# Norm statistics: squares added up over the feature tiles on GpSimd, one-column products, and the context's norm placed behind the latents' first products

## The chip, the cores and the metric

The kernel runs on one core of one Trainium2 chip. The metric is the device time of one execution in microseconds (us), lower is better. TensorE (PE) multiplies, VectorE (DVE), ScalarE (ACT) and GpSimd (POOL) do the element work, and each has its own in-order instruction queue; the queues of SyncE (SP), ACT and POOL also issue transfers.

## What is computed

Two layers of a diffusion trunk over 512 latent tokens and 256 context tokens, d_model 1024. Each layer has three token mixers behind one input projection, one output projection, and then a dense SwiGLU (layer 0) or an expert SwiGLU (layer 1). A modulated RMSNorm stands ahead of the input projection and ahead of the SwiGLU:

```
def rmsnorm(x, g):
    return x * lax.rsqrt(jnp.mean(jnp.square(x), axis=-1, keepdims=True) + EPS) * g
hl  = modulate(rmsnorm(x, norm1[l]), sh1, sc1);  hc  = modulate(rmsnorm(ctx, norm1[l]), csh1, csc1)
out_l, out_c = token_mixers(hl, hc, w_in[l], ..., w_out[l], ...)
x   = x + g1 * out_l;                            ctx = ctx + cg1 * out_c      # context in layer 0 alone
hl2 = modulate(rmsnorm(x, norm2[l]), sh2, sc2);  hc2 = modulate(rmsnorm(ctx, norm2[l]), csh2, csc2)
x   = x + g2 * channel_mixer(hl2, ...);          ctx = ctx + cg2 * channel_mixer(hc2, ...)
```

Shifts, scales and gates come from `w_mod` (12 groups of 512 columns a layer, called modulation groups here).

## The kernel before

The residual stream lies transposed: eight tiles `xr0` to `xr7` of 128 features by 768 tokens, the latents in columns 0 to 511 and the context in 512 to 767. Every fp32 product is made of three products of split operands: `hi` is a rounded copy (ACT, L207) and `lo` the rest, `raw - hi` (DVE, L208). So each 512 KB block of weights is loaded by SP into `raw`, split by ACT and DVE, and then used by PE in the lines L215 to L217. The buffers of `raw`, `hi` and `lo` rotate, three to five each, so a split also waits until the products of an older block are done.

There are two places that matter here, and both are in or behind layer 0.

**The tail of layer 0** (`tail`, 447 to 543 us). For the latents, then for the context: eight times (m = 0 to 7) load and split a block of `wout`, 24 products, and the residual update of `xr` on DVE (L687). Then `modnorm`: `stats` squares the eight `xr` tiles (odd ones on DVE in L337, even ones on ACT in L339), each square goes through a product with ones (L341) into PSUM, then a copy (L344), transposes (L231), a sum (L347), a root on DVE in 12 tiny instructions (`rsq`, L239 to L246), a diagonal (L352) and a product that spreads the root over the partitions (L357). After that come eight times a scaling (`ht`, DVE L362), `hh` (ACT L367) and `hl` (DVE L368), which are the split operands of the next products. The latents' norm is issued behind the latents' products and so runs on DVE and ACT while PE makes the context's.

**The feed-forward part** (`ffn`). Its blocks f = 0 and f = 1 make the latents' products of both blocks first and then the context's; later blocks do both at once. Beside them DVE makes modulation groups for later (`mod_acc`, L296). In the last chunk the down products (`wd4`, 18 matmuls for each of d = 0 to 7, residual update in L789) are made for the latents first and then for the context, each with its `modnorm` behind it; these norms are those of layer 1, and `project` of layer 1 begins with group 1 (four token tiles of the latents, 24 matmuls each, L221 to L223) and the channels (L215 to L217, latents and context).

What sets the order inside a queue is the order of the program text and the scheduler's priorities; each engine's queue is in order, so an instruction that waits holds up all behind it.

## Time and profile before

| | |
|---|---|
| median of 3 runs | 2162.6 us (2160.61 to 2163.68) |
| profiled execution | 2161.2 us |
| its span, first to last instruction | 2159.5 us, so 1.7 us lie around it |
| PE busy | 2027.9 us, 94% |
| DVE, ACT, POOL busy | 65%, 46%, 8% |
| granted TensorE clock, mean | 0.977 |

PE is busy nearly everywhere, so time is to be had where PE stands still or runs at a lower granted clock, and from products that are not made at all.

### The profile page before, as it was taken

How to read it: one execution, taken by the hardware profiler on the slowest of the kernel's cores; microseconds unless marked ns; L12 is line 12 of the kernel's file. 1: busy time of each engine (PE TensorE's matmuls, PEld its weight loads, DVE VectorE, ACT ScalarE, POOL GpSimd, SP SyncE). 2: the span in 40 equal slices, each digit the busy share in tenths (PEclk: the TensorE clock that was granted, in tenths of full speed). 3: DMA queues.
4: the chain of work that ended last, by engine and by line, in shares of the span. 5: the costliest groups of instructions: out<-in, count | busy, mean ns of one | idle time of the engine just before them, and what ended most of it. 6: DMA issues, size and time to landing. Idle time of an engine off the chain costs nothing. (4 is left out here: it accounts for less than half of the span.)

```text
span 2159.5 us, 33553 instructions
## 1 busy us (share of the span) xinstructions
PE 2027.9 (94%) x12470; PEld 1648.4 (76%) x12470; DVE 1401.9 (65%) x2501; ACT 990.2 (46%) x1728; POOL 179.9 (8%) x246
## 2 busy tenths in 40 slices
PE   6999899989999999999989999999889999999995
PEld 2988766767788888888858987778567777777774
DVE  4859845765885724242366599676676787766776
ACT  3665374533322212122235655754365576645554
POOL 0000231200000000000000004120110000001011
PEclk9999999999999999999989999999899999999998
DMA  7232543162654615131213324034597799667783
GB/s 271 91 121 85 184 144 129 39 198 62 203 204 137 200 35 200 30 98 58 91 48 92 120 81 127 27 104 150 172 308 269 257 350 325 217 218 250 238 291 118
DMA packets 120752, 342.45 MB, mean 159 GB/s; under 512 B 13104, under 2 KB 34592, under 8 KB 120576
## 3 DMA queue, kind: packets, MB, share of 16 engines
q1 hardware_dynamic: 80064, 271.75, 37.8%
q0 software_dynamic: 15248, 49.97, 6.9%
q10 hardware_dynamic: 25264, 18.42, 2.8%
q8 instruction: 106, 1.74, 0.3%
q14 instruction: 70, 0.57, 0.1%
HBM read 304.95 MB, written 35.14 MB: 157 GB/s over the span
## 5 line engine op out<-in xcount | busy, mean ns | idle before, releaser
L207 ACT ACTIVATE hi<-raw 128x1024 fp32r<-128x1024 f32 (+3 forms) x444 | 427.2, 987 | 332.5 <-PE ps L216 262.4
L208 DVE TENSOR_TENSOR lo<-raw,hi 128x1024 fp32r<-128x1024 f32 (+3 forms) x444 | 495.0, 1134 | 92.4 <-ACT hi L207 79.6
L217 PE MATMUL ps<-hh,lo 128*128 128x512 f32 (+1 forms) x1040 | 353.9, 340 | 2.5 <-DVE lo L208 2.5
L215 PE MATMUL ps<-hh,hi 128*128 128x512 f32 (+1 forms) x1040 | 355.1, 341 | 1.0 <-ACT hi L207 0.5
L216 PE MATMUL ps<-hl,hi 128*128 128x512 f32 (+1 forms) x1040 | 354.2, 341 | 0.0
L215 PEld LDWEIGHTS ps<-hh,hi 128*128 128x128 f32 x1040 | 198.1, 191 | 24.9 <-issue 1.7
L217 PEld LDWEIGHTS ps<-hh,lo 128*128 128x128 f32 x1040 | 198.0, 190 | 24.4 <-DVE lo L208 3.0
L216 PEld LDWEIGHTS ps<-hl,hi 128*128 128x128 f32 x1040 | 198.1, 191 | 21.4
L223 PE MATMUL ps<-lo,xh 128*128 128x512 f32 (+1 forms) x384 | 150.6, 392 | 9.5 <-DVE lo L208 4.6
L221 PE MATMUL ps<-hi,xh 128*128 128x512 f32 (+1 forms) x384 | 146.1, 380 | 2.2 <-ACT hi L207 2.2
L222 PE MATMUL ps<-hi,xl 128*128 128x512 f32 (+1 forms) x384 | 144.9, 377 | 0.0
L1273 DVE TENSOR_TENSOR sg<-sg,ps 128x512 f32<-128x512 f32 (+1 forms) x44 | 24.3, 553 | 154.7 <-PE ps L217 154.7
L216 PE MATMUL ps<-gl,hi 128*128 128x256 f32 (+1 forms) x352 | 119.4, 339 | 0.0
L215 PE MATMUL ps<-gh,hi 128*128 128x256 f32 (+1 forms) x352 | 118.9, 338 | 0.0
L217 PE MATMUL ps<-gh,lo 128*128 128x256 f32 (+1 forms) x352 | 118.5, 337 | 0.0
L223 PEld LDWEIGHTS ps<-lo,xh 128*128 128x128 f32 x384 | 72.4, 189 | 37.6 <-DVE lo L208 15.6
L221 PE MATMUL ps<-hi,hh 128*128 128x400 f32 (+2 forms) x272 | 92.2, 339 | 2.5 <-DVE ht L362 1.4
L223 PE MATMUL ps<-lo,hh 128*128 128x400 f32 (+2 forms) x272 | 89.0, 329 | 0.0
L222 PE MATMUL ps<-hi,hl 128*128 128x400 f32 (+2 forms) x272 | 88.9, 327 | 0.0
L1515 DVE TENSOR_REDUCE a_st<-S 128x1 f32<-128x768 f32 (+1 forms) x80 | 66.2, 844 | 33.9 <-PE S L1514 33.5
L296 DVE SCALAR_TENSOR_TENSOR macc<-mraw,sT,macc 128x512 f32<-128x512 f32 x112 | 80.0, 747 | 12.0 <-DMA mraw<-wmod 11.3
L1516 ACT ACTIVATE a_p<-S,a_st 128x768 f32<-128x768 f32 (+1 forms) x80 | 65.2, 817 | 45.8 <-DVE a_st L1515 40.5
(557 smaller groups left out, 4099.9 us busy)
## 6 DMA issues: line engine op xcount, KB each, us to landing
raw<-wmg SPq DMA_DIRECT2D x176, 512.0 KB
raw<-wmd SPq DMA_DIRECT2D x80, 512.0 KB
raw<-wmod SPq DMA_DIRECT2D x52, 512.0 KB
raw<-wgu SPq DMA_DIRECT2D x44, 512.0 KB
mraw<-wmod SPq DMA_DIRECT2D x44, 512.0 KB
raw<-wout SPq DMA_DIRECT2D x32, 512.0 KB
raw<-wt SPq DMA_DIRECT2D x24, 512.0 KB
raw<-wd SPq DMA_DIRECT2D x32, 256.0 KB
```

The lines of the kernel that those rows point to most:

```text
L207: self.nc.scalar.activation(hi, src, AF.Copy)
L208: self.nc.vector.tensor_sub(lo, src, hi.bitcast(F32))
L215: mm(out, wh, xh, start=start, stop=False)
L216: mm(out, wh, xl, start=False, stop=False)
L217: mm(out, wl, xh, start=False, stop=stop)
L221: mm(out, xh, wh, start=start, stop=False)
L222: mm(out, xl, wh, start=False, stop=False)
L223: mm(out, xh, wl, start=False, stop=stop)
L296: nc.vector.scalar_tensor_tensor(a, w, c, a, op0=OP.mult, op1=OP.add)
L1273: nc.vector.tensor_mul(s, s, pu)
L1515: nc.vector.tensor_reduce(st[:, 0, c + i:c + i + 1], s[:, :n], axis=AX.X, op=OP.min)
L1516: nc.scalar.activation(P[:, :n], s[:, :n], AF.Exp, bias=st[:, 0, c + i:c + i + 1], scale=-1.0, accum_out=st[:, 1, c + i:c + i + 1])
```

## The change

Squares all run on ACT (`square`), and GpSimd adds them up over the eight feature tiles into an accumulator (`nac0` for the latents, with the last square alone in `nac1`; `nacc` for the context). `rms` then makes one product of one column for each tile of 128 tokens and accumulator (eight for the latents, two for the context) and goes on with the root, the diagonal and the spreading product. Of the context's weight blocks (`wout` and `wd4`), three in four have their `lo` made on GpSimd. The context's norm of the tail is placed in `ffn` behind the first latents products, that of the feed-forward's end in `project` behind token tile 1 of group 1, with x read back from DRAM (`xres`). The latents' norm for layer 1 goes in two pieces of 256 columns. The writes of `xres` go from GpSimd's queue to SP's and ACT's. Modulation group 10 of layer 0 is no longer made on PE within the attention but as one more group on DVE in `ffn`.

```diff
+    def square(self, pool, acc, xs, k):
+        nc = self.nc
+        if k == 0 or k == 7 and len(acc) > 1:
+            nc.scalar.activation(acc[k // 7], xs, AF.Square)
+            return
+        sq = pool.tile([128, 512], F32, name="sq")[:, :xs.shape[-1]]
+        nc.scalar.activation(sq, xs, AF.Square)
+        nc.gpsimd.tensor_add(acc[0], acc[0], sq)
+
+    def rms(self, pool, acc, n, b, dg=None):
...
+        for t in range(m):
+            for j, a in enumerate(acc):
+                nc.tensor.matmul(q[:, t:t + 1], a[:, t * 128:t * 128 + 128], self.C("ones")[:, 0:1], start=j == 0, stop=j == len(acc) - 1)
+        self.rsq(pool, q[:, :m], [128, m], 1.0 / 1024, EPS, ss, "n")
...
+    def modnorm(self, pool, hh, hl, x, s, o, n, gain, modc, sh0, rs, w):
+        for c in range(0, n, w):
+            for k in range(8):
+                t = pool.tile([128, 512], F32, name="ht")[:, :w]
+                self.scaled(t, x, s, o + c, w, gain, rs[:, c:c + w], k)
+                self.shifted(t, hh, hl, s, o + c, w, modc, sh0, k)
...
-            attention = mix.attention(at, cat, list(range(4, 11)) if l == 0 else [])
+            attention = mix.attention(at, cat, list(range(4, 10)) if l == 0 else [])
...
+    def context():
+        sqs = [cv.tile([128, 4, 2, 64], F32, name="sq").rearrange("p t h d -> p (t h d)") for _ in range(2)]
...
+            nc.scalar.dma_start(xs[-1][:, :n * CTX].rearrange("p (d c) -> p d c", c=CTX), k.xsrc[1][:, d:d + n, LAT:])
+        rs = k.rms(cv, k.acc, CTX, "pg", sqs[1])
...
+                    if l == 1 and i == 1 and t == 1:
+                        context()
...
-                wh, wl = k.weight(A["wout"][l, m].rearrange("p k n -> p (k n)"))
+                wh, wl = k.weight(A["wout"][l, m].rearrange("p k n -> p (k n)"), eng=nc.gpsimd if s and m % 4 < 3 else None)
...
+                if not last:
+                    k.square(np_, acc, xm, m)
...
-        done, sums = [], {2: 4, 4: 4, 7: 4, 11: 4}
+        done, sums = [], {2: 4, 4: 4, 6: 4, 10: 4, 12: 2}
...
-            for i, g in ((0, 11), (1, 2), (1, 3), (1, 0), (1, 1), (1, 4), (1, 5), (1, 6), (1, 7), (1, 8), (1, 9)):
+            for i, g in ((0, 10), (0, 11), (1, 2), (1, 3), (1, 0), (1, 1), (1, 4), (1, 5), (1, 6), (1, 7), (1, 8), (1, 9)):
...
-                    up(fs, SEGS[:1])
+                    up(fs[:1], SEGS[:1])
+                    rs = k.rms(fp, k.acc, CTX, "pn", mp.tile([128, 512], F32, name="macc", bufs=6))
+                    for d in range(8):
+                        t = mp.tile([128, 512], F32, name="macc", bufs=6)[:, :CTX]
+                        k.scaled(t, x, 1, LAT, CTX, gain2, rs, d)
+                        k.shifted(t, hh, hl, 1, LAT, CTX, k.modc[l], 24, d)
+                    up(fs[1:], SEGS[:1])
...
-                    wh, wl = k.weight(A[f"wd{ci}"][d].rearrange("p f n -> p (f n)"), nff * 128)
+                    wh, wl = k.weight(A[f"wd{ci}"][d].rearrange("p f n -> p (f n)"), nff * 128,
+                                      nc.gpsimd if segs == (1,) and d % 4 < 3 else None)
...
-                            nc.gpsimd.dma_start(k.xsrc[1][:, d, :LAT], x[d][:, :LAT])
-                if lastc:
-                    o, n = SEGS[segs[0]]
-                    k.modnorm(np_, hh, hl, x, segs[0], o, n, gain, k.modc[1], 0)
+                            k.square(np_, acc, x[d][:, :LAT], d)
+                            nc.sync.dma_start(k.xsrc[1][:, d, :LAT], x[d][:, :LAT])
+                        elif lastc:
+                            k.square(np_, k.acc, x[d][:, LAT:], d)
+                            nc.scalar.dma_start(k.xsrc[1][:, d, LAT:], x[d][:, LAT:])
+                if segs == (0,):
+                    k.modnorm(np_, hh, hl, x, 0, 0, LAT, gain, k.modc[1], 0, k.rms(np_, acc, LAT, "pn"), 256)
```

Three places show what moves. The first is ACT at the start of layer 0's tail, in the kernel before; `xr_4795` is `xr0`, and `hi` are splits of `wout`, the first three of these for m = 3, 4 and 5 of the latents.

```order
L207 ACTIVATE hi<-raw 128x1024 x3
L339 ACTIVATE sq<-xr_4795 128x512
L207 ACTIVATE hi<-raw 128x1024 x5
L339 ACTIVATE sq<-xr_4799 128x512
L339 ACTIVATE sq<-xr_4803 128x512
```

The same place after, where `xr_4769` is `xr0` and `xr_4773` is `xr2`.

```order
L374 ACTIVATE nac_4839<-xr_4769 128x512
L377 ACTIVATE sq<-xr_4771 128x512
L377 ACTIVATE sq<-xr_4773 128x512
L207 ACTIVATE hi<-raw 128x1024 x4
L377 ACTIVATE sq<-xr_4775 128x512
L207 ACTIVATE hi<-raw 128x1024
```

The split for m = 3 now stands behind the square of `xr2`, which is there only when the products of m = 2 are done.

The second is DVE at the end of `ffn`, before: the last `lo` of `wd4` (128x768), the end of the root, and the beginning of the latents' norm.

```order
L208 TENSOR_TENSOR lo<-raw,hi 128x768
L246 SCALAR_TENSOR_TENSOR ss<-rqus,rqis 128x4
L352 TENSOR_TENSOR dg<-cst,ss 128x512
L789 SCALAR_TENSOR_TENSOR xr_4801<-ps,modc,xr_4801 128x256
L362 SCALAR_TENSOR_TENSOR ht<-xr_4795,gain_9693,pn 128x512
L362 SCALAR_TENSOR_TENSOR ht<-xr_4797,gain_9693,pn 128x512
```

The same engine after, at the one late `lo` that DVE still makes there, that of d = 7: `xr_4777` is `xr4`, and the rows are those of the second piece of 256 latents.

```order
L362 SCALAR_TENSOR_TENSOR ht<-xr_4777,gain_9697,pn 128x256
L362 SCALAR_TENSOR_TENSOR ht<-xr_4779,gain_9697,pn 128x256
L208 TENSOR_TENSOR lo<-raw,hi 128x768
L368 SCALAR_TENSOR_TENSOR hl_4761<-ht,modc_75,hh_4753 128x256
L368 SCALAR_TENSOR_TENSOR hl_4762<-ht,modc_75,hh_4754 128x256
L362 SCALAR_TENSOR_TENSOR ht<-xr_4781,gain_9697,pn 128x256
```

Of the 32 instructions of the latents' norm (16 `ht`, 16 `hl`), 26 now stand ahead of that `lo`, where before all stood behind it.

The third is PE where the feed-forward's end meets layer 1, before: the last down product of the context, the context's statistics, then token tile 0.

```order
L217 MATMUL ps<-gh,lo 128x256
L341 MATMUL pn<-sq,cst 32x256 x8
L231 MATMUL pn<-cst,pv 128x128 x2
L357 MATMUL pn<-dg,cst 128x256
L221 MATMUL ps<-hi,hh_4776 128x256
```

After, the token tiles follow the down products at once, and the context's two products stand between tiles 1 and 2 (the spreading product, not shown, between 2 and 3).

```order
L222 MATMUL ps<-hi,hl_4764 128x256
L223 MATMUL ps<-lo,hh_4756 128x256
L387 MATMUL pg<-cst,nacc 128x1 x2
L221 MATMUL ps<-hi,hh_4749 128x256
L222 MATMUL ps<-hi,hl_4757 128x256
```

The chain of statistics no longer stands between the last down product and the first token tile.

## Rows read from the trace of the kernel before

**Rows 1.** Busy time by engine in four stretches (PE, PEld, DVE, ACT, POOL, PEclk, DMA).
```profile
529.90:546.20 16.30, 8.71 (x44) 5.42 (x42) 9.33 (x26) 5.78 (x9) 0.00 (x0) 0.85 0.43 159
...
575.00:600.00 25.00, 25.00 (x167) 22.23 (x165) 23.98 (x39) 6.71 (x12) 0.00 (x0) 1.00 0.57 180
1115.30:1129.60 14.30, 5.29 (x21) 1.63 (x21) 11.56 (x35) 3.43 (x7) 0.57 (x2) 0.71 0.00 0
...
1107.20:1115.20 8.00, 8.00 (x69) 7.94 (x67) 7.70 (x13) 5.09 (x9) 0.53 (x1) 1.00 0.01 2
```

**Rows 2.** Timeline of the tail's latents: start, duration, engine, line, [idle before <-releaser].
```profile
469.00 2.25 ACT L207 ACTIVATE hi<-raw 128x1024 fp32r<-128x1024 f32 x2 [3.53 <-PE ps L216]
...
471.72 0.75 DVE L687 SCALAR_TENSOR_TENSOR xr<-ps,modc,xr 128x512 f32<-128x512 f32 x1 [0.61 <-PE ps L217]
...
472.38 3.49 DVE L208 TENSOR_TENSOR lo<-raw,hi 128x1024 fp32r<-128x1024 f32 x3
...
473.65 0.50 PE L217 MATMUL ps<-c6h,lo 128*128 128x512 f32 x1 [1.07 <-DVE lo L208]
```

**Rows 3.** Timeline of PE from the latents' end to the feed-forward's first products.
```profile
500.19 1.05 PE L341 MATMUL pn<-sq,cst 128*32 128x512 f32 x4
...
534.30 0.58 PE L217 MATMUL ps<-c6h,lo 128*128 128x256 f32 x1 [2.58 <-DVE lo L208]
...
538.63 0.62 PE L341 MATMUL pn<-sq,cst 128*32 128x256 f32 x4
...
546.21 0.80 PE L217 MATMUL ps<-hh,lo 128*128 128x512 f32 x1 [2.53 <-DVE lo L208]
```

**Rows 4.** Timeline, the same stretch: SP's transfers, ACT and DVE.
```profile
538.02 13.37 SPq L196 DMA_DIRECT2D raw<-wgu  x8
...
541.84 2.08 ACT L207 ACTIVATE hi<-raw 128x1024 fp32r<-128x1024 f32 x2
...
542.48 0.17 DVE L347 TENSOR_REDUCE ss<-pn 128x2 f32<-128x8 f32 x1 [1.62 <-PE pn L231]
...
544.93 1.23 DVE L208 TENSOR_TENSOR lo<-raw,hi 128x1024 fp32r<-128x1024 f32 x1
```

**Rows 5.** Timeline of PE, feed-forward's end to layer 1.
```profile
1088.38 0.39 PE L217 MATMUL ps<-gh,lo 128*128 128x512 f32 x1
...
1106.11 1.10 PE L357 MATMUL pn<-dg,cst 128*128 128x512 f32 x2
...
1129.61 0.78 PE L221 MATMUL ps<-hi,hh 128*128 128x256 f32 x1
...
1153.57 0.40 PE L215 MATMUL ps<-hh,hi 128*128 128x512 f32 x1
```

**Rows 6.** Timeline of DVE there, the context's norm.
```profile
1130.21 0.87 DVE L362 SCALAR_TENSOR_TENSOR ht<-xr,gain,pn 128x256 f32<-128x256 f32 x2 [1.38 <-PE pn L357]
...
1132.07 0.86 DVE L362 SCALAR_TENSOR_TENSOR ht<-xr,gain,pn 128x256 f32<-128x256 f32 x2
```

**Rows 7.** Groups by line and shape, POOL, whole span: count | busy, mean ns.
```profile
L1477 POOL TENSOR_TENSOR a_dg<-cst,a_st 128x512 f32<-128x512 f32 x20 | 21.1, 1054 | 125.0 <-PE t L1490 94.4 <-DVE a_st L1476 17.0 <-PE S L1514 10.2
L1841 POOL TENSOR_TENSOR ad<-cst,al 128x256 f32<-128x256 f32 x12 | 7.7, 644 | 22.8 <-DVE L L1860 21.5 <-DVE rquo L244 1.4
```

**Rows 8.** Timeline of POOL and DVE near the kernel's end, both at work.
```profile
2133.77 4.26 POOL L963 TENSOR_TENSOR cy<-tk,nfrow 128x512 f32<-128x512 f32 x3 [40.23 <-DVE tk L953]
...
2135.39 1.48 DVE L208 TENSOR_TENSOR xs<-y,xl 128x512 fp32r<-128x512 f32 x1
```

**Rows 9.** Groups by line and shape, DVE, 440 to 1140 us.
```profile
L296 DVE SCALAR_TENSOR_TENSOR macc<-mraw,sT,macc 128x512 f32<-128x512 f32 x112 | 80.0, 747 | 12.0 <-DMA mraw<-wmod 11.3
...
L208 DVE TENSOR_TENSOR lo<-raw,hi 128x512 fp32r<-128x512 f32 x36 | 24.6, 689 | 7.3 <-ACT hi L207 6.3
```

**Rows 10.** Timeline of PE in the attention, modulation group 10.
```profile
395.06 1.91 PE L265 MATMUL t<-raw,sT 128*32 128x512 f32 x12
...
402.25 1.11 PE L231 MATMUL t<-cst,m 128*128 128x128 f32 x4
```

More of the change, by code (lines that the diff above doesn't have):

```diff
@@ L545, in feat @@
         return k.proj(k.weight(A["wt"][l, m].rearrange("p k n -> p (k n)")), hh, hl, segs)
+    def context():
+        sqs = [cv.tile([128, 4, 2, 64], F32, name="sq").rearrange("p t h d -> p (t h d)") for _ in range(2)]
+        xs = []
+        for d, n in ((0, 3), (3, 3), (6, 2)):
+            xs.append(cv.tile([128, T], F32, name="cv") if d < 6 else sqs[0])
+            nc.scalar.dma_start(xs[-1][:, :n * CTX].rearrange("p (d c) -> p d c", c=CTX), k.xsrc[1][:, d:d + n, LAT:])
+        rs = k.rms(cv, k.acc, CTX, "pg", sqs[1])
+        for d in range(8):
+            t = xs[d // 3][:, d % 3 * CTX:d % 3 * CTX + CTX]
+            nc.vector.scalar_tensor_tensor(t, t, k.gain[:, 1, d:d + 1], rs, op0=OP.mult, op1=OP.mult)
+            k.shifted(t, hh, hl, 1, LAT, CTX, k.modc[l], 0, d)
     def group(i, w=None):
@@ L653, in tail @@
         hh, hl = htiles(hp)
+        k.acc = [hp.tile([128, CTX], F32, name="nacc")]
     xp = pb(es, "xp")
@@ L679, in tail @@
         for s, o, n in pieces:
+            acc = None if last else k.acc if s else [np_.tile([128, 512], F32, name=f"nac{i}", bufs=1) for i in range(2)]
             for m in range(8):
-                wh, wl = k.weight(A["wout"][l, m].rearrange("p k n -> p (k n)"))
+                wh, wl = k.weight(A["wout"][l, m].rearrange("p k n -> p (k n)"), eng=nc.gpsimd if s and m % 4 < 3 else None)
                 p = k.psum()
@@ L687, in tail @@
                 nc.vector.scalar_tensor_tensor(xm, like(p[:, :n], o), k.modc[l][:, s, 16 + m:17 + m], xm, op0=OP.mult, op1=OP.add)
-            if not last:
-                k.modnorm(np_, hh, hl, x, s, o, n, gain, k.modc[l], 24)
-            else:
+                if not last:
+                    k.square(np_, acc, xm, m)
+            if not last and s == 0:
+                k.modnorm(np_, hh, hl, x, s, o, n, gain, k.modc[l], 24, k.rms(np_, acc, n, "pn"), n)
+            elif last:
                 rs, = k.stats(np_, x, [(o, n)])
@@ L704, in tail @@
     if not last:
-        ffn(k, l, x, hh, hl)
+        ffn(k, l, x, hh, hl, gain)
         eb.close()
@@ L714, in tail, with ffn @@
     moe(k, l, x, hh, g2row, close)
-def ffn(k, l, x, hh, hl):
+def ffn(k, l, x, hh, hl, gain2):
     nc, A = k.nc, k.A
@@ L776, in ffn @@
             if lastc:
-                gain = k.gains(1, 0)
+                gain = k.gain = k.gains(1, 0)
                 em.close()
                 np_ = pa(es, "np4", 2)
+                acc = [np_.tile([128, 512], F32, name=f"nac{i}", bufs=1) for i in range(2)]
             for segs in ([(0,), (1,)] if lastc else [(0, 1)]):
                 for d in range(8):
-                    wh, wl = k.weight(A[f"wd{ci}"][d].rearrange("p f n -> p (f n)"), nff * 128)
+                    wh, wl = k.weight(A[f"wd{ci}"][d].rearrange("p f n -> p (f n)"), nff * 128,
+                                      nc.gpsimd if segs == (1,) and d % 4 < 3 else None)
                     for s in segs:
```

27 lines of the change are left out of this document (15 added, 12 removed).

## The prediction

> **What bounds the kernel now.** I read the totals by engine first: TensorE is busy almost all the time, so only a stretch in which it stands still, or runs at half its clock, or makes products that the change drops, can give time back. Then I looked for such stretches in the table of stretches and read the timeline of each engine in them. There are two, both behind a norm.
>
> In the tail of layer 0, TensorE works 8.71 of the 16.3 us from 529.9 to 546.2 at a mean granted clock of 0.85 [rows 1]. The timeline names the waits. The last context block stands 2.58 us for its `lo` from VectorE, which is busy with the latents' norm, and the feed-forward's third matmul, at 546.21, waits another 2.53 us for a `lo` [rows 3]. That second wait has a longer history: the loads of the new weights start at 538.02, as the last context products free their space, the ACT split follows at 541.84, and the `lo` only at 544.93, behind the root of the context's norm [rows 4].
>
> Between the feed-forward's end and layer 1, TensorE works 5.29 of the 14.3 us from 1115.3 to 1129.6 at 0.71 [rows 1]. There the reader is to see the chain of the context's statistics laid bare: the down products are made by 1115.3, and token tile 0 starts at 1129.61, although the latents that it needs have long been normalised [rows 5].
>
> **The tail, start.** ACT's squares of `xr1` and `xr2` now stand ahead of the split for m = 3. In the trace, that split begins at 469.00 and its third matmul comes at 473.65 [rows 2]. After the change the square can begin when the update of `xr2` ends, 471.72 + 0.75 = 472.47. I take 1.1 us for the split (2.25 for two), half of it for the square, which has half the columns, and 1.16 for `lo` (3.49 for three) [rows 2]: 475.3, so 1.7 us late. The row at 473.65 stands behind two matmuls of m = 4 that now come later (0.45 us). That is +2.1. After the wait of 2.58 us the 22 matmuls that were left of that block took from 534.30 to 538.6 [rows 3], 4.3 us where 2.6 do at full clock (0.119 each, below), so this wait may cost up to 1.6 more. I take +2.9, and the latents end at 503.0 instead of 500.1.
>
> **The tail, context.** Dropped are eight products with ones for the latents, their transposes, and the waits among them. What stays is 192 matmuls at 0.119 us (67 in 8.00 us, [rows 1]), 22.9 us, and one spreading product of 1.10 [rows 5]. The eight one-column products are not in the trace. From below they cost nothing; from above four records of 32 columns by 512 take 1.05 us [rows 3], so 0.26 each, 2.1 in all, which I take. The last context product then ends at 503.0 + 22.9 + 2.1 + 1.1 = 529.1 if no split is late, against 538.6 before [rows 3].
>
> Is a split late? GpSimd makes six of eight `lo`. Its rows give 0.644 us at 256 columns and 1.054 at 512 [rows 7], so 1.87 at 1024 along that line (an estimate). Three of these and four additions of 0.64 take 8.2 us for every four blocks, in which TensorE spends 11.4: there is room. The `lo` of the last block (m = 7) stays on VectorE, inside the latents' norm. That norm starts some 8 us after the latents' end, on a chain of the last update and square (1.4), products (up to 2.1 behind them), root (2.45, the time from 542.48 to 544.93 in [rows 4]), diagonal (0.7) and spreading product (1.1); its 16 instructions of 0.7 and the eight updates between them are then done by 525.6, and this `lo` by 526.7. The block needs its third matmul at 526.6. That is just in time, plus or minus 1.
>
> **The feed-forward's start.** The loads follow the context's products, so they move from 538.02 to 528.5. The first split followed 3.8 us behind [rows 4], at 532.3, and ends at 533.4; `lo` comes directly behind, as the root now stands later in VectorE's queue: 534.6. Before it was 546.21. So -11.6, the loss at the start included. It is kept if the context's operands are ready when the first context product comes, then at 559.2: norm statistics after the first latents products (545.5), spread at 547.7, eight pairs of `ht` and `hl` at about 1.1 us with ACT's part, 556.6. The slack is 2.6 us. Bounds: -13 (no loss of clock) and -8 (m = 7 or the operands 3.5 late).
>
> **The feed-forward's end.** The context's 8 x 18 matmuls take 17.1 us from the latents' end at 1088.6 [rows 5], with the 3.2 of norm products beside them, but for d = 7 the `lo` now stands behind 26 of the 32 instructions of the latents' norm. Their chain: last update and square to 1090.2, one-column products to 1092.4, root to 1095.3, diagonal to 1095.9, spread to 1097.1. Four instructions of 256 columns take 1.86 us [rows 6], 26 take 12.1, five updates between them 2.0, and this `lo` 0.95 (between 0.69 for 512 columns [rows 9] and 1.16): 1112.1. TensorE comes to it at 1107.3. It stands for 4.8 us, ends d = 7 between 1114.0 and 1115.5, and so gains nothing on the 1115.3 of before. The gain comes after: token tile 0 no longer waits for the context's chain. It waits for its own weight splits, behind the rest of the norm (2.8), and for two of them behind the square of `xr7` on ACT and six instructions of a rotary table on VectorE (2.0; 2.6 if all had the 0.43 of 256 columns): 1119.5 to 1120. Tile 0 ends about 1120.5, tiles 1 to 3 (2.86 each at full clock, plus 1.6 for the norm's products and up to 2 for a low clock) about 1131, channel 0 about 1138.5, against 1153.57 [rows 5]. That is -15; bounds -9 (each split 3 us later) and -17. The context's operands come just in time: root after tile 1, spread after tile 2 (1127.5), eight pairs in 7.4 [rows 6], 1135.
>
> **The rest.** Group 10 leaves the attention: 12 of its 16 records take 1.91 us, so all 2.6, and its transposes 1.11 [rows 10], 3.7 together. It had a transfer to wait for as well, but other waits lie there too, so I take -3.5 (0 to -5). On VectorE it comes back as 16 instructions of 0.747 [rows 9], 12 us beside TensorE, and the later sum of two more accumulators costs one product and four transposes, +1.0 (by the 1.11 of [rows 10]). The writes of `xres` from other queues, at nothing: they run beside other work and nobody reads them for 10 us, but the context's read-back needs them, by about 1121.
>
> The odd squares go from VectorE to ACT at nothing but the wait at the start: ACT works 5.78 of the 16.3 us and 3.43 of the 14.3 in the two stretches [rows 1].
>
> **Sum.** -3.5 - 11.6 - 15 + 1.0 = -29.1 on the profiled 2161.2, so 2132; the median of the runs stands 1.4 above this profile, so 2134. The bounds of the terms alone give 2129 to 2147.
>
> **Rivals.** First, *GpSimd holds VectorE up*. During the two latents' norms GpSimd has 8.2 and some 7 us of work. If VectorE stood for half to all of it, both last `lo` would be 4 to 7 us later, and 9 to 12 of the gain would go: 2144. In the one place where both work, VectorE took 1.48 us for two where two alone take 1.38, and GpSimd 1.42 each against 1.054 [rows 7 to 9]. So the rows say that GpSimd loses a third and VectorE a tenth. The Trainium skill says otherwise ("SBUF — State Buffer", section "Who interferes with whom"): a VectorE instruction with two SBUF inputs and a GpSimd one that reads SBUF exclude each other, and the loser blocks for the whole of the other. By that rule it would be this rival or the slower one below; the row at 2135.39 does not show a whole block of VectorE, which would have cost it about 1 us.
>
> Second, *VectorE becomes the bound in the feed-forward*. It is busy 23.98 of 25 us from 575 to 600 [rows 1]. The 12 us of group 10 and the context's norm come into this stretch, and if they don't fit beside, a `lo` is late by up to that much: about +10, 2144. Against it: before, no wait of TensorE is seen there (25.00 of 25), and the modulation's work can lag until its sum.
>
> Third, the slower side: *VectorE starves GpSimd*. If GpSimd got nothing while a norm runs (14 us each), the `lo` of the context's middle blocks would wait for the norm's end, and TensorE with them, some 14 us in each place and up to 5 more at half clock behind it. -29.1 + 28 + 10 is +9: 2171. It decides from 12 us in each place on (24 + 10 - 29 = +5). For it speaks that GpSimd is the one that loses in [rows 8]; but 1.42 against 1.054 is a third, not all, and on six `lo` and four additions makes about 4.
>
> Fourth, *the change doesn't do what it says*: the context's operands come so late behind their cover that TensorE waits for them instead, in both places. My two chains leave 2.6 and 0 us of slack, and 29 us would have to be lost in them: each would have to be twice as long as its eight pairs of 7.4 to 9 us. 2161.
>
> **Chances.** Forecast (2123 to 2141) 0.62, first rival 0.17, second 0.10, third 0.06, fourth 0.05. The range 2122 to 2150 leaves out the last two and the ends of the first. From these, faster by over 0.2% (about what a measurement of this kernel can tell from no change) 0.89, within 0.2% 0.04, slower 0.07.
>
> **What would show it.** Right: a wait of about 2 us at m = 3 near 473; none over 1 us at the last context block; 31.6 us from the tail's last latents product to the feed-forward's third matmul (46.1 before); a wait of 4 to 5 us at d = 7 before layer 1, and token tile 0 within 1 us of the last down product. Wrong: GpSimd's `lo` of 1024 columns well above 2 us, VectorE's `hl` longer beside them, or waits of TensorE between 560 and 650.

## The result, and the profile after

The changed kernel takes 2132.65 us (median of four runs, 2131.47 to 2134.87), the kernel before beside it 2161.63 (2160.61 to 2163.68): a ratio of 0.9868, interval 0.9853 to 0.9884. Forecast were 2134 and 2122 to 2150. The profiled execution took 2131.47 with a span of 2129.9 us, so 29.6 less than the span before.

Where they went is read by lengths: the start of one and the same instruction in both timelines, and the difference from one to the next (us).

| stretch | before | after | change | forecast |
|---|---|---|---|---|
| start to the first product of the tail | 445.8 | 442.5 | -3.3 | -3.5 |
| latents of the tail | 54.1 | 59.2 | +5.1 | +2.9 |
| context of the tail | 38.5 | 30.0 | -8.6 | -12.4 |
| to the feed-forward's third matmul | 7.8 | 6.6 | -1.2 | -2.1 |
| to the end of the latents' down products | 542.2 | 543.7 | +1.5 | +1.0 |
| from there to the channels | 65.2 | 51.6 | -13.6 | -15 |
| channels of layer 1 after channel 0 | 32.0 | 27.5 | -4.5 | 0 |
| mixers of layer 1, last 105 to 109 us | 108.8 | 104.7 | -4.1 | 0 |
| all the rest | 865.1 | 864.2 | -0.9 | 0 |

The total is as forecast and the parts are not: the tail gave less than half of what was expected (-4.7 instead of -11.6 in its three rows), and two stretches gave 8.6 us that the sum did not have. First the tail and the feed-forward's first products, in the timeline of PE (it answers to [rows 2, 3]).

```profile
471.84 0.50 PE L215 MATMUL ps<-c6h,hi 128*128 128x512 f32 x1 [2.45 <-ACT hi L207]
...
473.39 0.50 PE L217 MATMUL ps<-c6h,lo 128*128 128x512 f32 x1 [0.82 <-DVE lo L208]
...
527.77 0.39 PE L217 MATMUL ps<-c6h,lo 128*128 128x256 f32 x1 [2.20 <-DVE lo L208]
...
533.99 0.61 PE L387 MATMUL pn<-cst,nacc 128*128 128x1 f32 x4 [1.68 <-POOL nacc L378]
535.48 0.70 PE L215 MATMUL ps<-hh,hi 128*128 128x512 f32 x1 [0.88 <-ACT hi L207]
...
538.18 0.79 PE L217 MATMUL ps<-hh,lo 128*128 128x512 f32 x1 [1.58 <-DVE lo L208]
```

The first two rows are the block m = 3, which now waits for its split, 2.45 and 0.82 where [rows 2] has one wait of 1.07. The third is the last context block: its wait of 2.20 has hardly shrunk from the 2.58 of [rows 3]. The fourth was not foreseen: the context's one-column products stand ahead of the feed-forward's first product and wait for GpSimd's last addition.

Why the last context block's `lo` is late shows in the timelines of DVE and POOL. `ht` reads the spread root from PSUM; `hl` has its tensors in SBUF.

```profile
514.70 1.40 DVE L362 SCALAR_TENSOR_TENSOR ht<-xr,gain,pn 128x512 f32<-128x512 f32 x2
...
516.41 2.63 DVE L368 SCALAR_TENSOR_TENSOR hl<-ht,modc,hh 128x512 fp32r<-128x512 f32 x2
...
524.65 1.40 DVE L368 SCALAR_TENSOR_TENSOR hl<-ht,modc,hh 128x512 fp32r<-128x512 f32 x2
...
526.37 1.35 DVE L208 TENSOR_TENSOR lo<-raw,hi 128x1024 fp32r<-128x1024 f32 x1
...
514.93 2.41 POOL L208 TENSOR_TENSOR lo<-raw,hi 128x1024 fp32r<-128x1024 f32 x1 [0.70 <-ACT hi L207]
517.30 1.19 POOL L378 TENSOR_TENSOR nacc<-nacc,sq 128x256 f32<-128x256 f32 x1
...
1086.62 0.15 DVE L245 SCALAR_TENSOR_TENSOR rqun<-rqun,rqxn 128x4 f32<-128x4 f32 x1
...
1087.20 1.70 DVE L245 SCALAR_TENSOR_TENSOR rqun<-rqun,rqxn 128x4 f32<-128x4 f32 x1
...
1089.33 1.67 DVE L245 SCALAR_TENSOR_TENSOR rqun<-rqun,rqxn 128x4 f32<-128x4 f32 x1
...
1087.03 1.85 POOL L208 TENSOR_TENSOR lo<-raw,hi 128x768 fp32r<-128x768 f32 x1 [2.22 <-ACT hi L207]
1089.18 1.80 POOL L208 TENSOR_TENSOR lo<-raw,hi 128x768 fp32r<-128x768 f32 x1 [0.30 <-ACT hi L207]
```

Two `hl` take 1.40 where GpSimd begins only behind the first of them (524.65), and 2.63 beside GpSimd's `lo` and addition (516.41); the `ht` at 514.70 take their usual 1.40 beside the same `lo`. The last five rows are plainer still, in the latents' root at the feed-forward's end. An instruction of four columns takes 0.15 at 1086.62, and 1.70 when GpSimd's `lo` has begun just ahead of it; it ends at 1088.90, the `lo` at 1088.88. The next pair ends at 1091.00 and 1090.98. So VectorE stands until GpSimd's whole instruction is done. This is what the Trainium skill says ("SBUF — State Buffer", section "Who interferes with whom"), and the trace agrees with it, not with the reading of [rows 8] in the prediction. That reading took the VectorE row at 2135.39 for two instructions, 1.48 against 1.38. The row has x1, and one instruction of this shape takes 0.69 [rows 9]: VectorE lost 0.79 there. GpSimd's second and third instruction there, taken singly, show why (the first took 1.31):

```profile
2135.04 1.28 POOL L963 TENSOR_TENSOR cy<-tk,nfrow 128x512 f32<-128x512 f32 x1
2136.29 1.74 POOL L963 TENSOR_TENSOR cy<-tk,nfrow 128x512 f32<-128x512 f32 x1
```

The second ended at 2136.32, and VectorE's instruction 0.55 later, at 2136.87. So the kernel before had shown the standing already, and of GpSimd's three only the last was longer.

The timeline of PE from the feed-forward's end into layer 1 answers to [rows 5].

```profile
1092.06 2.05 PE L392 MATMUL pn<-ndg,cst 128*128 128x512 f32 x2 [3.25 <-DVE ndg L390]
...
1108.05 0.39 PE L217 MATMUL ps<-gh,lo 128*128 128x256 f32 x1 [2.79 <-DVE lo L208]
...
1110.86 0.41 PE L221 MATMUL ps<-hi,hh 128*128 128x256 f32 x1
...
1133.40 0.40 PE L215 MATMUL ps<-hh,hi 128*128 128x512 f32 x1
```

The spreading product waits 3.25 for the root (of which 1.54 + 1.51 is the standing just seen), the down product d = 7 waits 2.79 for the late `lo`, and token tile 0 follows at 1110.86 with no wait ahead of it; before, it started 14.5 us behind the last down product.

Busy time and clock by stretch, first of before, then of after (PE, PEld, DVE, ACT, POOL, PEclk, DMA): the latents of the tail, the channels behind channel 0, and the mixers; of after also two parts of the latents' stretch, and the context.

```profile
445.81:499.88 54.07, 49.56 (x226) 39.60 (x225) 30.86 (x55) 15.95 (x24) 1.63 (x3) 0.97 0.59 185
...
1153.57:1185.57 32.00, 29.59 (x173) 25.76 (x171) 20.92 (x41) 15.05 (x27) 0.13 (x1) 0.95 0.22 66
...
1384.43:1493.23 108.80, 101.69 (x1053) 87.00 (x1049) 81.85 (x190) 51.85 (x112) 16.27 (x25) 0.94 0.36 111
```

```profile
442.48:501.65 59.17, 53.08 (x225) 41.66 (x225) 28.05 (x52) 19.54 (x30) 14.75 (x11) 0.91 0.51 165
...
442.48:450.00 7.52, 6.70 (x28) 4.99 (x27) 5.38 (x13) 4.21 (x8) 0.55 (x1) 0.56 0.54 154
471.84:480.00 8.16, 7.34 (x24) 5.62 (x25) 3.77 (x3) 1.84 (x2) 0.41 (x1) 0.79 0.56 193
...
501.65:531.62 29.97, 27.51 (x211) 26.59 (x210) 21.99 (x39) 14.63 (x22) 16.23 (x10) 0.95 0.22 68
...
1133.40:1160.95 27.55, 27.55 (x172) 24.65 (x171) 22.24 (x48) 17.49 (x29) 0.13 (x1) 1.00 0.39 112
...
1359.13:1463.83 104.70, 97.94 (x1053) 83.94 (x1049) 81.91 (x190) 51.90 (x112) 16.27 (x25) 0.98 0.36 115
```

In the latents of the tail PE stands 6.1 us instead of 4.5 and is busy 3.5 us longer with the same products, at 0.91 of the clock instead of 0.97: of the +5.1 only 1.6 is waiting, the rest is the lower clock. It is low (in part 1.2 GHz, the lower of its two levels) in two places: behind the waits at m = 3, with a mean of 0.79 from 471.84 to 480, which costs 1.7 us (0.21 of 8.16), and in the tail's first 7.5 us, with 0.56, 3.3 us. Before, it was 1.00 in both, and 0.83 from 450 to 460, 1.7 us. In the mixers it stands 6.8 instead of 7.1, so all but 0.3 of the -4.1 is clock: 0.98 against 0.94, for the same 1053 matmuls. The channels are PE's alone now (27.55 of 27.55); before, it stood 2.4 us there, at these two places of its timeline, and lost the rest to a clock of 0.95.

```profile
1159.64 0.36 PE L215 MATMUL ps<-hh,hi 128*128 128x256 f32 x1 [0.44 <-DVE cv L395]
...
1164.71 0.55 PE L231 MATMUL pg<-cst,cv 128*128 128x128 f32 x3 [1.97 <-ACT cv L1571]
```

GpSimd's work by groups, 440 to 1140 us (count | busy, mean ns):

```profile
L378 POOL TENSOR_TENSOR nac<-nac,sq 128x512 f32<-128x512 f32 x12 | 16.1, 1344 | 269.4 <-ACT sq L377 254.1 <-issue 13.3 <-DVE lo L208 1.9
L208 POOL TENSOR_TENSOR lo<-raw,hi 128x1024 fp32r<-128x1024 f32 x6 | 14.8, 2471 | 12.7 <-ACT hi L207 12.7
L378 POOL TENSOR_TENSOR nacc<-nacc,sq 128x256 f32<-128x256 f32 x14 | 12.3, 881 | 20.7 <-ACT sq L377 20.7
L208 POOL TENSOR_TENSOR lo<-raw,hi 128x768 fp32r<-128x768 f32 x6 | 11.0, 1835 | 8.3 <-ACT hi L207 8.3
```

A `lo` of 1024 columns takes 2.47 on the mean (2.35 to 2.41 in five of the six), not the estimated 1.87: the line through [rows 7] was drawn through instructions whose operands are a constant and a repeated column. With two whole operands, 512 columns took 1.28 in the kernel before already (2135.04 above), against 1.054 in [rows 7].

### The profile page after: what moved, and what is told of

The parts are those of the page before. It is cut to its first block, busy times and chain, and to the rows that moved or that the text cites. A ratio compares the mean times of both kernels' runs of the same rounds, so it can differ in the third digit from the quotient of the medians.

```text
span 2129.9 us, 33569 instructions
## 1 busy us (share of the span) xinstructions
PE 2006.1 (94%) x12422; PEld 1641.6 (77%) x12422; DVE 1398.6 (66%) x2501; ACT 996.4 (47%) x1748; POOL 228.5 (11%) x276
## 5 line engine op out<-in xcount | busy, mean ns | idle before, releaser
L208 DVE TENSOR_TENSOR lo<-raw,hi 128x1024 fp32r<-128x1024 f32 (+2 forms) x432 | 482.8, 1137 | 88.1 <-ACT hi L207 74.7
L223 PEld LDWEIGHTS ps<-lo,xh 128*128 128x128 f32 x384 | 72.5, 189 | 38.5 <-DVE lo L208 18.5
L296 DVE SCALAR_TENSOR_TENSOR macc<-mraw,sT,macc 128x512 f32<-128x512 f32 x126 | 89.2, 748 | 14.4 <-DMA mraw<-wmod 13.7
```

What stands on the lines that cost most here:

```text
L208: (eng or self.nc.vector).tensor_sub(lo, src, hi.bitcast(F32))
L223: mm(out, xh, wl, start=False, stop=stop)
L296: nc.vector.scalar_tensor_tensor(a, w, c, a, op0=OP.mult, op1=OP.add)
```

## The experiments

Every kernel is the changed one with one edit or several, timed beside the kernel before on its chip. The unedited kernel was timed again too, so that the spread of chips and executions can be read.

**The context's `lo` on VectorE.** GpSimd keeps the additions.

```diff
-  eng=nc.gpsimd if s and m % 4 < 3 else None)
+  eng=None)
-  nc.gpsimd if segs == (1,) and d % 4 < 3 else None)
+  None)
```

> The changed kernel (2132.65 us) with every `lo` of the context's wout and wd4 blocks made on VectorE again; additions stay on GpSimd. Theory 1 (a VectorE instruction with two SBUF inputs waits for the whole of a GpSimd one: in the changed kernel's trace the root's L245 took 1.70 instead of 0.16 us and ended with GpSimd's lo, and hl of 512 columns took up to 1.2 instead of 0.74): the 3.25 us wait ahead of the latents' spreading product at the feed-forward's end goes below 1 us, the 2.79 us wait at d = 7 too, as its lo then stands ahead of the norm; in the tail three lo of 1.2 us come into the norm and about 2.8 us of blocking go, so the last block's wait of 2.20 stays within 1.5 of that. 4 to 6 us faster than the changed kernel: 2127 to 2129. Rival (GpSimd's relief of VectorE is what carries the gain): the waits at the last blocks grow to 5 us or more in both places, 6 to 10 us slower: 2139 to 2143.

Measured: 2140.21 (2136.88 to 2140.84), ratio 0.9893 (0.9877 to 0.9908). PE's timeline at the third product of the tail's context block m = 6, the spreading product, and the context's statistics:

```profile
529.87 0.58 PE L217 MATMUL ps<-c6h,lo 128*128 128x256 f32 x1 [4.30 <-DVE lo L208]
...
1096.86 1.10 PE L392 MATMUL pn<-ndg,cst 128*128 128x512 f32 x2 [0.70 <-DVE ndg L390]
...
1112.89 1.02 PE L387 MATMUL pg<-cst,nacc 128*128 128x1 f32 x4 [4.39 <-POOL nacc L378]
1113.77 0.56 PE L221 MATMUL ps<-hi,hh 128*128 128x256 f32 x1
```

In the tail GpSimd's help is worth having: without it PE waits for a `lo` one block sooner and 2.1 us longer, and the context takes 33.0 instead of 30.0. At the feed-forward's end the root runs freely (L392 waits 0.70 instead of 3.25), d = 7 doesn't wait, and the context's down products are 7.8 us shorter. Then the context's statistics come into PE's queue with their last addition missing, wait 4.39, and to the channels only 0.9 us is left. They stand here ahead of token tile 0 (1113.77), directly behind the last down product, and not between tiles 1 and 2 as in the changed kernel: with the edit the order in PE's queue changed too. So this run doesn't give the price of GpSimd's `lo` at this place alone; without the 4.39, and if no other wait took its place, it would be 38.0 us to channel 0 by an estimate (42.35 - 4.39), 5 less than in the changed kernel. The time is neither what the theory said nor, with a wait of 4.30 in one place and none in the other, by the rival's way.

**Both context norms in their old place,** statistics and GpSimd as changed.

```diff
-  if not last and s == 0:
+  if not last:
...
-  if l == 1 and i == 1 and t == 1:
-      context()
```

> The changed kernel with both context norms back where they stood, at the end of the tail and of the feed-forward; squares, additions and one-column products as changed. Theory 1 (statistics and placing each carry part): in the tail little is lost, 0 to 3 us, since the root stands ahead of the first lo in both; at the feed-forward's end token tile 0 waits for the context's chain again, square, addition, product, root 2.4, diagonal, spread, some 6 us, and TensorE runs at the low clock behind it, up to 3: 8 to 13 us slower than the changed kernel, 2141 to 2146. Rival (the placing is nearly all of it): 18 us or more slower, 2150 and above, so that the new statistics alone bring 10 us or less.

Measured: 2146.88 (2144.41 to 2148.91), ratio 0.9926 (0.9908 to 0.9944). From the tail's latents to the feed-forward's third matmul it takes 38.2 us, where before takes 46.3 and the changed kernel 36.5: there the rest of the change (statistics and GpSimd's `lo`) brings 8.1 and the placing 1.7. From the latents' down products to channel 0 it is the other way round: 56.5 against 56.8 and 43.2, so the placing brings 13 and the rest nothing. The median is 14.2 and 11.7 above those of the unedited kernel, at the upper end of the theory's 8 to 13 and short of the rival's 18. PE's timeline shows why:

```profile
1118.78 1.01 PE L387 MATMUL pn<-cst,nacc 128*128 128x1 f32 x4 [2.36 <-POOL nacc L378]
...
1123.94 1.19 PE L392 MATMUL pn<-ndg,cst 128*128 128x256 f32 x2 [4.16 <-DVE ndg L390]
...
1131.66 0.39 PE L221 MATMUL ps<-hi,hh 128*128 128x256 f32 x1 [1.99 <-DVE ht L362]
```

The chain of addition, root, diagonal and norm is bare again. The channels behind channel 0 take 28.2 us here, so all but 0.7 of their 4.5 us don't come from the placing.

**The latents' squares of the tail two blocks later,** so that the split for m = 3 stands ahead of the square of `xr2`.

```diff
+  late.append((acc, xm, m))
+  if len(late) > (0 if s else 2):
+      k.square(np_, *late.pop(0))
```

> The changed kernel with the latents' squares in the tail written two blocks later, so that ACT's split for m = 3 stands ahead of the square of xr1. Theory 1: the waits of 2.45 and 0.82 us at m = 3 shrink to the 1.07 of the kernel before, and the low clock behind them (0.74 from 475 to 480) goes: the latents end 3 to 4 us earlier, 2129 to 2130. Rival (the wait is set by the rotation of the weight buffers, which the squares only happen to stand beside): the waits stay, 2132 to 2133.

Measured: 2134.06 (2131.95 to 2136.03), ratio 0.9867 (0.985 to 0.9884). At m = 3 one wait of 2.27 stays (`473.88`, for `lo`) in place of 2.45 and 0.82, the granted clock is 1.00 behind it (473.88 to 482.00), and the latents take 56.7 instead of 59.2. VectorE's timeline shows what that `lo` waits for:

```profile
471.61 5.57 DVE L208 TENSOR_TENSOR lo<-raw,hi 128x1024 fp32r<-128x1024 f32 x3
```

Three `lo` take 5.57 where [rows 2] has 3.49, beside two additions of GpSimd that begin at 471.48 and 472.95: the hold-up of VectorE in a third place. In the median nothing is seen; the two of the unedited kernel (2132.65, and 2135.18 below) are as far apart. The feed-forward has a wait of 1.69, on ACT, among transposes of a modulation group.

**Group 10 back in the attention.**

```diff
-  list(range(4, 10)) if l == 0
+  list(range(4, 11)) if l == 0
-  sums = [], {2: 4, 4: 4, 6: 4, 10: 4, 12: 2}
+  sums = [], {2: 4, 4: 4, 7: 4, 11: 4}
```

> The changed kernel with modulation group 10 of layer 0 made on TensorE in the attention again. Theory 1: the tail's first product starts 3.3 us later (445.8 instead of 442.5), the feed-forward loses its extra sum and ends 1 to 2.2 us sooner: 1 to 2.5 us slower than the changed kernel, 2133.5 to 2135. Rival (group 10 on VectorE costs as much beside the feed-forward as it saves in the attention): no slower, 2131 to 2133.

Measured: 2137.91 (2134.77 to 2138.44), ratio 0.9889 (0.9872 to 0.9906). The tail starts at 446.26. Over the profiles of all kernels timed at least four times it starts at 443.8 on the mean with the group moved (ten, 441.8 to 446.0) and at 446.3 with the group in the attention (three, 445.8 to 446.9): -2.6, not -3.5. The feed-forward, from its first down product to the latents' last, takes 474.5 on the mean of the ten and 471.6 of the three: +2.9. Seven of the ten have a wait of 0.6 to 2.1 there, on ACT, among transposes of a modulation group, and the three have none. By these lengths the move pays nothing; the median, 2.7 to 5.3 above those of the unedited kernel, would have it pay, but the intervals of the ratios overlap.

**The context's one-column products held behind the feed-forward's first product,** by a column of ones that ACT writes after it.

```diff
+  if f_ == 0 and n == LAT:
+      nc.scalar.activation(oc, pg[:, 0:1], AF.Identity, bias=k.C("ones")[:, 0:1], scale=0.0)
...
-  nc.tensor.matmul(q[:, t:t + 1], a[:, t * 128:t * 128 + 128], self.C("ones")[:, 0:1], start=j == 0, stop=j == len(acc) - 1)
+  nc.tensor.matmul(q[:, t:t + 1], a[:, t * 128:t * 128 + 128], one or self.C("ones")[:, 0:1], start=j == 0, stop=j == len(acc) - 1)
```

> The changed kernel with the context's one-column products held back by a dependence: the ones column is a tile that ACT writes from the first feed-forward product of the latents (and, in layer 1, from token tile 0). Theory (in the changed kernel these products stand in TensorE's queue ahead of the first feed-forward product and wait 1.68 us there for GpSimd's last addition, and the root behind them stands ahead of the new weights' lo on VectorE): the stretch from the last context product to the third feed-forward matmul falls from 6.6 to about 5 us, the low clock behind it may go as well; nothing changes before layer 1, where they already stand behind tile 1. 1.5 to 4 us faster than the changed kernel. Rival (the transfer of the new weights alone sets that stretch, 3.6 us from its issue to its split): within 0.5 us of 6.6, no faster.

Measured: 2136.26 (2135.33 to 2139.44), ratio 0.9891 (0.9873 to 0.9909). The third matmul comes 5.5 us behind the tail's context instead of 6.6, the length that the prediction had; what is left there is the split behind its load (a wait of 3.73 for `hi`). In the total this is not seen, against the theory's 1.5 to 4.

**Blocks 0 and 4 on VectorE, the last one on GpSimd.**

```diff
-  eng=nc.gpsimd if s and m % 4 < 3 else None)
+  eng=nc.gpsimd if s and m % 4 else None)
-  nc.gpsimd if segs == (1,) and d % 4 < 3 else None)
+  nc.gpsimd if segs == (1,) and d % 4 else None)
```

> The changed kernel with the lo of blocks 0 and 4 of the context's wout and wd4 on VectorE and the other six, the last one among them, on GpSimd (the change has 3 and 7 on VectorE). Theory (the last block's lo stands in VectorE's queue behind the latents' norm): the waits of 2.20 us at m = 7 and of 2.79 us at d = 7 go below 1 each, with up to 2 us of low clock behind the first; the 3.25 us wait for the root, which GpSimd's lo holds up, stays. 4 to 6 us faster than the changed kernel. Rival (GpSimd's last lo is held up as long by VectorE's hl as VectorE's lo was by the queue): the waits stay over 2 us, within 1 us of the changed kernel.

Measured: 2139.11 (2134.93 to 2141.92), ratio 0.9893 (0.9874 to 0.9912). Both last-block waits are gone, and the 3.25 at the spreading product behind the feed-forward stays, as the theory said. But others have come: 2.03 at the tail's spreading product (0.26 in the changed kernel), and these two in PE's timeline of layer 1, the first inside token tile 0. From the latents' down products to the end of the channels it takes 85.7 us instead of 79.1.

```profile
1114.07 1.01 PE L387 MATMUL pg<-cst,nacc 128*128 128x1 f32 x4 [3.00 <-POOL nacc L378]
...
1132.87 0.50 PE L215 MATMUL ps<-hh,hi 128*128 128x512 f32 x1 [2.97 <-ACT sq L1382]
```

**No GpSimd at all:** the first edit, and the additions on VectorE.

```diff
-  nc.gpsimd.tensor_add(acc[0], acc[0], sq)
+  nc.vector.tensor_add(acc[0], acc[0], sq)
```

> The changed kernel without GpSimd: every addition and every lo on VectorE. Theory 1 (GpSimd and VectorE exclude each other, so what GpSimd takes over is partly paid on VectorE): no instruction of the root or of hl is longer than alone (0.16, 0.74), TensorE's waits at the last blocks are as in the run with lo on VectorE, about 4.3 us in the tail and none at d = 7, plus four to seven additions of 0.42 in each norm: 2 to 5 us slower than that run. Rival (the relief by GpSimd is worth its whole busy time): the norms end some 10 us later each, 10 us or more slower than that run.

Measured: 2134.41 (2132.63 to 2136.51), ratio 0.9875 (0.9858 to 0.9892). The tail's context is the longest of all variants, 34.3 (the `lo` of m = 5 makes PE wait 4.47), and the way from the latents' down products to channel 0 the shortest of those with the whole computation, 41.1 against 43.2, with the spreading product's wait down to 0.16. The context's one-column products stand ahead of token tile 0 here too and wait 3.90. From the tail's latents to the feed-forward's third matmul it takes 40.3, against 46.3 before and 36.5 in the changed kernel, so GpSimd's part there is 3.8 of the 9.8. The time is that of the changed kernel, and not above that of the run with `lo` on VectorE (ratio 0.9893): theory and rival both missed. All that GpSimd does for these norms can't be seen in the total.

**Four edits together:** late squares, held products, and GpSimd's `lo` for six blocks of `wout` (not 0 and 4) and none of `wd4`.

```diff
-  eng=nc.gpsimd if s and m % 4 < 3 else None)
+  eng=nc.gpsimd if s and m % 4 else None)
-  nc.gpsimd if segs == (1,) and d % 4 < 3 else None)
+  None)
```

> Four edits on the changed kernel together: the latents' squares in the tail two blocks later, the context's one-column products held back as in the run before, the lo of wout blocks 0 and 4 on VectorE and the others on GpSimd, and all lo of wd4 on VectorE. Theory: the stretches add up as they did one by one: tail latents 2.5 us less, tail context 2 to 4 less, feed-forward's start 1.5 to 3 less, feed-forward's end (wait of the root and of d = 7 gone, the products held behind tile 0) 3 to 6 less: 9 to 14 us faster than the changed kernel, 2119 to 2124. Rival (the waits replace each other): 2127 or more.

Measured: 2135.84 (2134.58 to 2136.59), ratio 0.9883 (0.9866 to 0.9899); the hoped-for ten did not come, as the rival had it. The root is delayed in the tail (a wait of 2.03), token tile 0 waits 1.60 and 1.59 for its `lo`, and the context's products 3.26 for the ones.

**The changed kernel, unedited.**

> The changed kernel once more, unedited, for the stretches that differ between profiles by the clock alone. Theory (of the changed kernel's 29 us some 4 come from a stretch of layer 1's mixers, 104.7 us long in its profile and 108.8 in the kernel before, that the change does not touch, and that is 104.6 to 109.2 long in the other runs): its median lies between 2133 and 2137, and that stretch is at one of the two lengths, 104.7 or 108.8. Rival (the stretch is shorter because of the change): 104.7 again, and a median of 2132 to 2133.

Measured: 2135.18 (2132.39 to 2136.79), ratio 0.9871 (0.985 to 0.9893). The same waits stand at the same places (2.45 and 0.82, 2.19, 1.76, 3.25, 2.79). The latents of the tail take 58.0 instead of 59.2. The mixers of layer 1 in its profile:

```profile
1357.42:1466.89 109.47, 102.35 (x1052) 87.25 (x1048) 81.88 (x190) 51.79 (x112) 16.23 (x25) 0.94 0.34 110
```

That is 109.5 us at 0.94, where the first profile of the same code had 104.7 at 0.98.

**Late squares, held products in the feed-forward alone, `lo` and additions of its end on VectorE, group 10 in the attention.** The new line of it:

```diff
-  nc.gpsimd.tensor_add(acc[0], acc[0], sq)
+  (eng or nc.gpsimd).tensor_add(acc[0], acc[0], sq)
```

> The changed kernel with what helped singly: the latents' squares in the tail two blocks later, the one-column products of the context held behind the feed-forward's first product, at the feed-forward's end all lo and all additions on VectorE, and modulation group 10 back in the attention. By the stretches of the earlier runs: tail latents 56.7 (59.2), tail context 30, feed-forward's start 5.5 (6.6), feed-forward 471.0 (473.3 to 476.7), its end to the channels 41 (43.2), the attention 2 to 3 longer: 3 to 7 us faster than the changed kernel on the same chip. Rival (the gains replace each other, and group 10 costs more in the attention): within 2 us of it.

Measured: 2134.0 (2129.81 to 2136.73), ratio 0.9863 (0.984 to 0.9886): not told from the changed kernel. From the latents' down products to channel 0 it takes 41.2, with a wait of 3.97 for the last addition, again ahead of token tile 0.

**The latents' norm for layer 1 in one piece.**

```diff
-  k.rms(np_, acc, LAT, "pn"), 256)
+  k.rms(np_, acc, LAT, "pn"), 512)
```

> The changed kernel with the latents' norm for layer 1 in one piece of 512 columns. Theory (the pieces cost VectorE 32 instructions of 0.43 instead of 16 of 0.70, and the lo of d = 7 stands behind most of them): the norm ends 2 to 3 us sooner, and token tile 0 and the d = 7 wait with it, 1 to 3 us faster. Rival (the first piece's early end is what token tiles 0 and 1 use): tile 0 waits for the whole norm, 1 to 3 us slower.

Measured: 2137.91 (2133.48 to 2140.25), ratio 0.9885 (0.9861 to 0.9909). d = 7 waits 3.39 instead of 2.79; to channel 0 it takes 42.7, not more than the 43.2 of two pieces. The pieces bring nothing that can be seen.

**GpSimd's `lo` as an instruction with one input,** a plain copy. It leaves out the subtraction of `hi`, so its results are not the reference's.

```diff
+  if eng is None:
+      self.nc.vector.tensor_sub(lo, src, hi.bitcast(F32))
+  else:
+      eng.tensor_copy(lo, src)
```

> The changed kernel with GpSimd's lo as a plain copy of the raw weights, so that the subtraction of hi is left out there and GpSimd reads one SBUF input. Theory (GpSimd reading SBUF at all holds up a VectorE instruction with two SBUF inputs): the root's L245 is still long when it meets a copy, and ends with it, and hl too, by the length of the copies. Rival (only a GpSimd instruction with two SBUF inputs does so): L245 at 0.16 and hl at 0.74 beside the copies, and the 3.25 us wait before the spreading product is gone even where copies run.

Measured: 2127.77 in one run. Timelines of DVE and POOL (its lines stand three further on, L248 is the L245 of the others):

```profile
510.35 0.48 DVE L733 SCALAR_TENSOR_TENSOR xr<-ps,modc,xr 128x256 f32<-128x256 f32 x1
...
1084.74 0.47 DVE L248 SCALAR_TENSOR_TENSOR rqun<-rqun,rqxn 128x4 f32<-128x4 f32 x1
...
1086.62 1.28 DVE L393 TENSOR_TENSOR ndg<-cst,nss 128x512 f32<-128x512 f32 x1
...
509.95 1.39 POOL L211 CAST lo<-raw 128x1024 fp32r<-128x1024 f32 x1 [6.55 <-issue]
...
1084.37 0.83 POOL L211 CAST lo<-raw 128x768 fp32r<-128x768 f32 x1 [3.11 <-PE ps L220]
...
1086.53 0.83 POOL L211 CAST lo<-raw 128x768 fp32r<-128x768 f32 x1 [1.33 <-PE ps L220]
```

The four-column instruction at 1084.74 ends at 1085.21, the copy at 1085.20; the diagonal, 0.69 in the changed kernel, takes 1.28 with a copy begun just ahead of it. So a GpSimd instruction with one input holds VectorE up as well, to its end; it is only over sooner. The Trainium skill ("SBUF — State Buffer", section "Who interferes with whom") makes no difference between one input and two on GpSimd's side, and the trace agrees. An update that reads PSUM takes its 0.48 (510.35) in the middle of a copy that began at 509.95. The spreading product waits 1.11 instead of 3.25, and the tail's last context block doesn't wait any more.

## Why the prediction was right, point by point

**The total** was right within 1.4 us, and partly by luck. The placing came as described at the feed-forward's end. The tail's term was mis-sized by 6.9 us, and what it lost came back in two stretches that the sum didn't have. Of the five signs of being right, two came: the wait at m = 3, and token tile 0 within 1 us of the last down product. Three missed: the last context block waits 2.20 and not under 1, the stretch of 31.6 us is 36.5, and d = 7 waits 2.79 and not 4 to 5. Two of the three signs of being wrong came as well, GpSimd's `lo` at 2.47 and longer `hl` beside it. So the first rival was at work, while the time was the forecast's.

**The tail's start.** Said was a wait of about 2 at m = 3 and +2.9 in all. The waits are 3.27 where [rows 2] had 1.07, so +2.2 there; the latents' +5.1 is 1.6 of standing and 3.5 of lower clock. The mis-sized term is the clock, of which the sum had 0.8 (2.9 less 2.1): behind the wait it cost 1.7, and some 1.6 more the sum had nowhere, the low clock of the tail's first products (3.3) less that of before from 450 to 460 (1.7). Why it is low there was not tried, and 1.2 of the 5.1 is missing from the second profile of the same code (58.0). With the squares later the latents take 1.3 to 2.5 us less; the wait that stays there is VectorE behind GpSimd's additions.

**The tail's context.** The step that failed is "just in time, plus or minus 1" for the `lo` of m = 7. PE waited 2.20 for it, because "GpSimd loses a third and VectorE a tenth" was wrong: it rests on [rows 8], where one instruction of VectorE was read as two. Six `hl` beside GpSimd took 2.77 longer than at 524.65 (0.60, 1.23 and 0.94 for the three pairs), and that alone is more than the wait. The context took 30.0 instead of 26.1: 2.5 of standing, the rest clock. Shorter GpSimd instructions remove the wait, which bears this out. Without any GpSimd PE waits 4.47 two blocks sooner and the context takes 34.3, so in the tail GpSimd still spares VectorE more than it takes. The first rival's mechanism is real, at about half the price that it was given (2.8 and 3.05 of standing instead of 4 to 7 in each place).

**The feed-forward's start.** The root "stands later in VectorE's queue" was wrong. The one-column products stand in PE's queue ahead of the first feed-forward product, wait 1.68, and the root comes ahead of the first `lo` on VectorE. The order of the program's text had been taken for that of the queue. Held back, the third matmul comes after the 5.5 us that the sum had. Its price was 1.1.

**The feed-forward's end.** -13.6 against -15. Two errors nearly cancel: the down products end later than forecast (28.8 behind the latents' against 25.4 to 26.9), with 3.25 lost at the spreading product, and token tile 0, forecast to wait 4 to 5 us for its splits, waits 0.46 inside it. The wait at d = 7 is 2.79 instead of 4.8, since PE itself comes later. The run with the old placing confirms the forecast's core, that the gain comes behind the down products and from the placing.

**Group 10.** -3.5 and +1.0 were forecast; over thirteen profiles it is -2.6 and +2.9. The second rival, VectorE as the bound in the feed-forward, is seen in this at most: PE waits 0.2 there in the first profile after, not at all in the second, and up to 2.06 (in the run with four edits) in those with the group moved.

**What the sum didn't have.** The channels' 4.5 us are the two waits of 0.44 and 1.97 and the clock behind them; all but a wait of 0.42 they are gone with the old placing too, and with GpSimd left out, with group 10 back, and with the norm in one piece. So none of these parts alone removes them; which one does was not tried. The mixers' 4.1 us are no effect of the change: the same code shows both lengths. Without them the profiled gain is about 25.5 us, and the two medians of the changed kernel stand 29.0 and 26.3 below the kernel before.

**The third and fourth rival** did not occur: no context block before the last waits for GpSimd, and the context's operands are there in time in both places.

What stays open is why no variant with the whole computation has a median below 2132. With a cure for one wait the lost time stands a few us further on, in the next instruction that needs VectorE or an addition; from the latents' down products to channel 0 the kernels timed at least four times, all but the old placing and the last `lo` on GpSimd, lie between 41 and 44 us. In part this is the order in PE's queue, which differs in three of them (the runs with `lo` on VectorE, without GpSimd, and with `lo` and additions of the end on VectorE): the context's one-column products stand ahead of token tile 0 there and wait 3.9 to 4.4 us. That VectorE's queue as a whole is the bound there fits, but no run took work away from it alone.

## What to carry to other kernels

Before work is given to GpSimd beside a busy VectorE, ask which VectorE instructions have two inputs in SBUF: each of them may stand for the whole of GpSimd's instruction, so short GpSimd instructions harm less than long ones, and a chain of tiny VectorE instructions is the worst neighbour. And leave the helper out once: here GpSimd's whole part could not be seen in the total. Where a bare chain of statistics stands decides what pays: at the feed-forward's end placing it behind other products brought 13 us and the rest of the change nothing, in the tail it was 1.7 and 8.1. Look up in each engine's queue where the chain really stands, after every edit. And compare lengths of stretches over several executions before a gain is credited to a change.

## What the runs showed of the hardware that had not been expected

VectorE's four-column instruction took 1.70 us instead of 0.15 behind a GpSimd instruction of 1.85 that had begun 0.17 earlier, and ended 0.02 after it. GpSimd loses as well: additions of 256 columns took 1.20 and 1.19 in the tail (513.02, 517.30), among `hl` of VectorE, and 0.72 to 0.74 in six of seven at the feed-forward's end. In the run with `lo` on VectorE one took 3.37 (528.17), while `hl` and two `lo` followed each other on VectorE without a gap, the two `lo` at 2.35 together, hardly longer than alone (1.22 at 520.25).

The same code ran the mixers of layer 1 at a mean granted clock of 0.98 in one execution and 0.94 in another, 4.8 us apart.

A product of one column costs hardly less than one of 256. For the context four records took 0.61 us at 533.99, and four of the 256-column products with ones that they replace 0.62 (538.63 in [rows 3]). Against 512 columns it is about half: 14 records in 1.62 at 503.65, four in 1.05 [rows 3]. For the context the gain is that 4 records stand where 16 did.
